# A second gate and up block by seven products instead of eight, with priorities for what it needs first

## The chip, the core and the metric

The kernel runs on one core of a Trainium2 chip. The metric is device time in microseconds (us), here the median of three runs. Beside the times there is one profiled execution; all rows of the profile come from it, in microseconds from the start of its span.

## What is computed

The kernel is one step of a hybrid transformer layer for 128 context tokens and 512 latent tokens, 640 in all, of width 1024. What matters here is its last third, the feed-forward part, for both kinds of tokens:

```python
x = x + g1 * mix
h2 = _rms(x, norm_ffn) * (1 + sc2) + sh2
gate, up = jnp.split(h2 @ w_gate_up, 2, axis=-1)
x = x + g2 * ((jax.nn.silu(gate) * up) @ w_down)
```

The gate and the up projection have 2816 columns each. `mix` is the result of attention and of a short convolution, after an output projection. All of it is in float32.

## The kernel before

**Matmuls in three parts.** A float32 operand is kept as a sum of two tiles: a high part, which ScalarE (ACT) copies into a rounded format (L148, or L1020 for tokens), and a low part, the rest, which VectorE (DVE) subtracts (L149, L1021). TensorE (PE) then multiplies high by high, high by low and low by high (`mm3`, L151 to L154). Making the two parts is called a split.

**Output projection** (L1039 to L1083). Tokens stand in five tiles of 128, the context first (`TORD`). The loop over `j` takes the two halves of the 1024 columns, the inner loop the five token tiles. In the second half, each token tile is added to `x`, normed (`x2n`), and in the next turn transposed by PE (`h2_turn`, L955, L961). The results leave PSUM with the second modulation (L968 on ACT; for the last tile half of them on DVE, L966) and make up `h2`, which has the tokens along its columns.

**Token operands.** `h2` is cut into four quarters: the first digit is the half of the 1024 features, the second the half of the 640 tokens, low (LO) or high (HI), 320 each. B11, B12, B21 and B22 are these quarters, split (`b_plain`). T1 = B12 - B11, T2 = B22 - T1, T3 = B22 - B12 and T4 = B21 - T2 are made of them by DVE (L1034) and split as well (`b_sums`). The high half is made in two pieces: its first 192 columns as soon as their tokens are there, and its last 128 columns (`two[1]`), which belong to the last token tile, later.

**Gate and up blocks.** The feed-forward columns are taken in 22 blocks of 128. For block `f`, A11 and A12 are the gate weights of the two feature halves, A21 and A22 the up weights. Each quarter of the result can be had from two products of a weight operand and a token operand, eight for a block (`plain`, L1103: four for LO, four for HI). Or the block takes seven products, in the manner of Strassen and Winograd: A11·B11, S1·T1, S2·T2, A12·B21, S3·T3, A22·T4 and S4·B22, with the weight sums S1 = A21 + A22, S2 = S1 - A11, S3 = A11 - A21 and S4 = A12 - S2 (`op_load`, L204). A product is twelve matmuls of 128x128 by 320. The first `NPLAIN` blocks (56: two of them) are plain, the others are done in `ff_a` to `ff_e` and `ff_end`: the products accumulate in shared PSUM banks, which ACT copies out in between (L1130), and DVE adds the parts (L1143, L1159, L1162, L1169) and multiplies silu(gate) by up (L1113, L1163, L1171). The texts call the blocks the first (`f` 0), the second (`f` 1), the third (`f` 2) and so on.

**What sets the order.** PE runs its instructions in the order of the program. On the other engines the order is planned when the kernel is built: among the instructions that are ready, the one that comes first in the program is taken, and inside `early(n)` (L144) an instruction counts as if it stood `n` places earlier. Weights come through a planned list (`plan`, L284 to L308): `W(key)`, at each product, also issues the steps that stand up to `AOP` = 9 places further on, so operands are made ahead. They are not issued before their phase (`phase[0]`; 2 up to the start of the blocks, 3 from L1225 on). The raw weights of a block are loaded by SyncE (L222) in two pieces, gate and up, into three buffers (`WFB`); a split operand takes one of four buffers of tag `wh` or of tag `wl`, in turn, and these are shared with the output weights.

The order of the first blocks is written out in L1216 to L1228: the first 192 high columns of the token operands and of their sums; four LO products of the first block; transposes of the last token tile; its columns of B12 and B22; four LO products of the second block; the last columns of T1 to T4; four HI products of each block. From the third block on each runs as `ff_a`, `ff_c`, `ff_end` of the block before, `ff_d`, `ff_b`, `ff_e` (L1229 to L1240).

Of the kernel before, what the change touches and what calls it, by code (L numbers as in the profile page):

```python
# [11 lines left out]
AF = mybir.ActivationFunctionType  # L12
# [6 lines left out]
NL = 4  # L19
# [29 lines left out]
GCUT = [0, 6, 12, 17, 22]  # L49
GB = 3  # L50
SOP = [20, 0]
CPP = 50
GSP = 30
FEND = 2
AOP = 9
NPLAIN = 2
QEV = '00001'
PPO = ''
RSP = 0
# [5 lines left out]
BHD = ("B21", "B22")  # L65
TL = 1
G2N = 0
DSI = 0
PT = 2
PRB = 4  # L70
PHB = 2
# [1 line left out]
BP = 300  # L73
# [15 lines left out]
def build(ctx, tc, x_prompt, x_sample, c, cache_k, cache_v, c_ctx, norm_mix, norm_ffn, w_ada, b_ada,  # L89
# [54 lines left out]
    def early(n):  # L144
        return tc.high_priority(n)
# [46 lines left out]
    def op_load(e):  # L192

        f, name = e[0][1:]
        g, u = (order[place[x, f]][5] for x in "gu")
        a11, a12, a21, a22 = g[:, 0:4], g[:, 4:8], u[:, 0:4], u[:, 4:8]
        if name[0] == "S":
            if name == "S1":
                sums[f] = T("sx", (P, 2, 4, P), F32, 2)
            s13, s24 = sums[f][:, 0], sums[f][:, 1]  # L200
            src, x, y, op = {"S1": (s13, a21, a22, ALU.add), "S2": (s24, s13, a11, ALU.subtract),
                             "S3": (s13, a11, a21, ALU.subtract), "S4": (s24, a12, s24, ALU.subtract)}[name]
            with early(SOP[f >= NPLAIN]):
                (pool if f < SPO else dve).tensor_tensor(src, x, y, op)  # L204
        else:
            src = {"A11": a11, "A12": a12, "A21": a21, "A22": a22}[name]
        w = T(("wh", "wl")[ops[0] % 2], (P, 2, 4, P), F32R, WHB)
        ops[0] += 1
        with early(SOP[f >= NPLAIN]):
            split(w[:, 0], w[:, 1], src)  # L210
        e[5] = w

# [70 lines left out]

    GROUPS = [list(range(a, b)) for a, b in zip(GCUT, GCUT[1:])]  # L284
    PLAIN, PRODS = ("A11", "A12", "A21", "A22"), ("A11", "S1", "S2", "A12", "S3", "A22", "S4")

    def plan_raw(f, x, ph=3):
        col = f * P + (DFF if x == "u" else 0)
# [2 lines left out]
    def plan_ops(f, names, ph=3):  # L291
        for x in names:
            plan(("op", f, x), None, ph, "op")

    G2KP = {0: (0,), 1: (1,), 2: (2, 3)}
    for gi, grp in enumerate(GROUPS):
        for f in grp:
            ph = 2 if f < NPLAIN else 3
            plan_raw(f, "g", ph)
            plan_raw(f, "u", ph)  # L300
            plan_ops(f, PLAIN if f < NPLAIN else PRODS, ph)
        for j in range(2):
            for i0 in range(0, len(grp), 2):
                n = len(grp[i0:i0 + 2])
                plan(("d", grp[i0], j), wd[:, grp[i0]:grp[i0] + n, j * 512:(j + 1) * 512], 2)
                if gi == 0 and j == 0:
                    for kp in G2KP[i0 // 2]:
                        plan(("ada", 5, 1, kp), wa[:, 2 * kp:2 * kp + 2, 5 * D + 512:6 * D], 2, "f")  # L308
# [469 lines left out]
    rA = [None] * NT  # L778
# [119 lines left out]
    def att_rms(t):  # L898
        sps = PB((P, 1))
        for p in range(4):  # L900
            pe.matmul(sps, osq[t][:, p], ones[:, 0:1], start=(p == 0), stop=(p == 3))
        rA[t] = rstd_of(sps, 1, 1.0 / 512, tag="rA")
# [40 lines left out]
    phase[0] = 2  # L943


    if DSI:
        act.activation(warm, warm, AF.Silu)
    h2 = [T("gT", (P, 4, TOK), F32, GB) for _ in range(2)]
    LO, HI = slice(0, HALF), slice(HALF, TOK)
    x2 = [None] * NT  # L950
# [4 lines left out]
    def h2_turn(t):  # L955
        cc = 1 if t == CTX else 0
        for g in range(2):
            tp = PB((P, 4, P))
            for i in range(4):
                k = 4 * g + i  # L960
                pe.transpose(tp[:, i], x2n[t][:, k * P:(k + 1) * P], ident)  # L961
            for i in range(4):
                k = 4 * g + i
                dst, a, b = h2[g][:, i, TS[t]], modA[1][:, k, cc:cc + 1], modB[1][:, k, cc:cc + 1]
                if i >= 4 - H2E[t]:
                    dve.tensor_scalar(dst, tp[:, i], a, b, ALU.mult, ALU.add)  # L966
                else:
                    act.activation(dst, tp[:, i], AF.Identity, bias=b, scale=a)  # L968
# [54 lines left out]
    def b_plain(names, part):  # L1023
        for x in names.split():
            b_put(x, quarter(x, part), part)

    def b_sums(part):
        n = part.stop - part.start
        b11, b12, b21, b22 = (quarter(x, part) for x in ("B11", "B12", "B21", "B22"))
        last = None  # L1030
        for x in ("T1", "T2", "T3", "T4"):
            w = T("tr", (P, 4, 192), F32, 3)[:, :, :n]
            y, z = {"T1": (b12, b11), "T2": (b22, last), "T3": (b22, b12), "T4": (b21, last)}[x]
            dve.tensor_tensor(w, y, z, ALU.subtract)  # L1034
            b_put(x, w, part)
            if x != "T3":
                last = w

    for j in range(2):  # L1039
        cols = slice(j * 512, (j + 1) * 512)  # L1040
        for n, t in enumerate(TORD):
            cc = 1 if t == CTX else 0
            c0 = t * P + (2 if t == CTX else 0)
            ms = [mix_ctx if t == CTX else mix_half(of[t]), mix_half(yf[:, :, c0:c0 + P])]
            ab = PS2()
            for half in range(2):
                for p in range(4):
                    wh, wl = W(("o", j, 2 * half + p // 2))
                    mm3(ab[:, half], ms[half][0][:, p], ms[half][1][:, p], wh[:, p % 2], wl[:, p % 2],
                        p == 0, p == 3)  # L1050
                if j == 0 and CRP == f"{n}{'me'[half]}":
                    next(ada_gen, None)
                    conv_rms()
            if j == 1 and n:
                h2_turn(TORD[n - 1])
                with early(BP):
                    if n == 2:
                        b_plain("B11 B21", slice(0, 256))
                    if n == 3:
                        b_plain("B11 B21", slice(256, HALF))  # L1060
            if j == 0 and n == 1:
                att_rms(NL - 1)
            if j == 0 and G2N <= n < 4 + G2N:
                g2_step(0, n - G2N)
            if j == 1 and n == 0:
                g2_out(0)
            if j == 0:
                x2[t] = T("x2", (P, D), F32, NT)
                sp.dma_start(x2[t], x_dram[t])
            with early(XP[j]):  # L1070
                m = T("mix", (P, 512), F32, 2)
                act.activation(m, ab[:, 1], AF.Copy, scale=rB[t])
                dve.scalar_tensor_tensor(m, ab[:, 0], rA[t], m, ALU.mult, ALU.add)
                e = pool if j == 0 and n < PX else dve
                e.tensor_tensor(m, m, g1[cc][:, cols], ALU.mult)
                e.tensor_tensor(x2[t][:, cols], m, x2[t][:, cols], ALU.add)
            if j == 1:
                with early(XP[j]):
                    x2n[t] = T("x2n", (P, D), F32, 1)
                    ss = T("ss", (P, 1), F32, 6)  # L1080
                    act.activation(x2n[t], x2[t], AF.Square, accum_out=ss)
                    r = rstd_of(ss, 1, 1.0 / D)
                    dve.tensor_scalar_mul(x2n[t], x2[t], r)  # L1083
# [49 lines left out]
    def ff_a(f):  # L1133
        b1 = FB()
        prod(b1, f, "A11", "B11")
        cg = T("cg", (P, TOK), F32, 2)
        st[f] = [b1, copy_of("p1", b1), cg, None, None, None, None]
# [76 lines left out]
    for gi, grp in enumerate(GROUPS):  # L1214
        for f in grp:
            if f == 0:  # L1216
                two = slice(0, 192), slice(192, HALF)
                b_plain("B12 B22", two[0])
                b_sums(two[0])
                for x in range(NPLAIN):  # L1220
                    plain(x, ("B11", "B21"), LO)
                    if x == 0:
                        h2_turn(TORD[-1])
                        b_plain("B12 B22", two[1])
                        phase[0] = 3  # L1225
                b_sums(two[1])
                for x in range(NPLAIN):
                    plain(x, ("B12", "B22"), HI)  # L1228
            elif f >= NPLAIN:  # L1229
                ff_a(f)  # L1230
                if f - 1 in st and FEND == 1:
                    ff_end(f - 1)
                ff_c(f)
                if f - 1 in st:
                    ff_end(f - 1)
                ff_d(f)
                ff_b(f)
                ff_e(f)
                if f == grp[-1] or FEND == 0:
                    ff_end(f)  # L1240
        down(gi, grp)
        for f in grp:
            del gT[f]
# [52 lines left out]
```

## Time and profile before

| | us |
|---|---|
| median of 3 runs | 763.05 |
| lowest, highest | 762.94, 763.66 |
| the profiled execution | 762.58 |
| its span, first to last instruction | 760.8 |

The mean granted clock of TensorE in the profiled execution is 0.996. In the profile a row names the line, the engine, the operation, the tile written and the tiles read, with partitions and elements. In rows of the timeline the first number is the start, the second the duration (of all merged instructions, where a count above 1 stands at the end); in square brackets is the engine's idle time just before and what ended it. A merged row ends with its last instruction. In rows by stretch the first three columns are the stretch and its length, then the busy time of each engine with its number of instructions, then the granted clock of TensorE (1.00 is full), the busy share of the DMA engines and GB/s. An instruction's duration is longer than the distance to the next one where the engine overlaps the two.

### The profile page before, as it was taken

The page shows a single profiled execution, that of the slowest core. Times are in us where ns is not written, and L with a number is a line of the kernel's source. Part 1 is how long each engine was busy: PE and PEld are TensorE (multiplying, and loading weights), DVE is VectorE, ACT ScalarE, POOL GpSimd, SP SyncE. Part 2 cuts the span into 40 slices and gives each one's busy share as a digit, 9 for nine tenths or more (in the row PEclk, how much of TensorE's full clock was granted, in tenths as well). Part 3 has the DMA queues.
Part 4 walks back from the last instruction along what each step waited for, and adds up shares of the span by engine and source line. Part 5 has one row for each costly group of instructions (what it writes and reads, how often), then busy time and mean ns, then how long its engine had stood idle before and what let it go on. Part 6 is the DMA issues. An engine that isn't in the chain of part 4 may idle for free.

```text
span 760.8 us, 11888 instructions
## 1 busy us (share of the span) xinstructions
PE 738.9 (97%) x4580; PEld 662.7 (87%) x4580; DVE 560.1 (74%) x1009; ACT 373.8 (49%) x712; POOL 48.2 (6%) x77
## 2 busy tenths in 40 slices
PE   4999999999999999989999999999999999999997
PEld 3778988989999887789998789998889998899986
DVE  5566987676666798899879678884578866788653
ACT  5455776656665445865552135553125541255410
POOL 3105201011010130000000000000000000000000
PEclk9899999999999999999999999999999999999999
DMA  9994134433424443121325223223113132222312
GB/s 290 298 255 133 44 110 133 133 91 120 144 90 147 153 171 111 35 77 56 110 89 180 82 62 103 83 86 114 52 56 110 58 111 73 67 87 81 112 55 84
DMA packets 102350, 84.52 MB, mean 111 GB/s; under 512 B 4527, under 2 KB 82675, under 8 KB 102293
## 3 DMA queue, kind: packets, MB, share of 16 engines
q1 hardware_dynamic: 100980, 83.39, 36.0%
q8 instruction: 36, 0.59, 0.3%
q10 hardware_dynamic: 1056, 0.26, 0.2%
q0 software_dynamic: 256, 0.11, 0.1%
q14 instruction: 22, 0.17, 0.1%
HBM read 79.68 MB, written 2.75 MB: 108 GB/s over the span
## 4 chain that ended last, share of the span: by engine, by line
PE 81%; DVE 9%; ACT 2%; issue 2%; DMA 2%; SPq 1%; POOL 1%; POOLq 0%; ACTq 0%; DVEq 0%
PE pf L152 17%; PE pf L153 17%; PE pf L154 17%; PE pc L675 3%; PE pc L676 3%; PE pc L677 3%; PE pc L377 2%; PE po L832 2%; PE ps L789 2%; PE pt L815 2%; PE ps L152 2%; PE ps L153 2%; PE ps L154 2%; DMA af<-in_w_ada_dram 1%; POOL rs L162 1%
## 5 line engine op out<-in xcount | busy, mean ns | idle before, releaser
L148 ACT ACTIVATE wh<-wf 128x1024 fp32r<-128x1024 f32 (+1 forms) x76 | 64.1, 843 | 92.0 <-PE pf L154 63.8
L152 PE MATMUL pf<-wh,gT 128*128 128x512 f32 (+1 forms) x225 | 88.0, 391 | 0.0
L153 PE MATMUL pf<-wl,gT 128*128 128x512 f32 (+1 forms) x225 | 87.6, 389 | 0.0
L154 PE MATMUL pf<-wh,gT 128*128 128x512 f32 (+1 forms) x225 | 87.6, 389 | 0.0
L149 DVE TENSOR_TENSOR wl<-wf,wh 128x1024 fp32r<-128x1024 f32 (+1 forms) x42 | 49.2, 1172 | 27.3 <-ACT wh L148 24.4
L675 PE MATMUL pc<-hH,wh 128*128 128x320 f32 x192 | 61.1, 318 | 0.0
L677 PE MATMUL pc<-hH,wl 128*128 128x320 f32 x192 | 59.4, 309 | 0.0
L676 PE MATMUL pc<-hL,wh 128*128 128x320 f32 x192 | 59.3, 309 | 0.0
L153 PEld LDWEIGHTS pf<-wl,gT 128*128 128x128 f32 x225 | 42.2, 187 | 9.9 <-DVE wl L149 0.2
L154 PEld LDWEIGHTS pf<-wh,gT 128*128 128x128 f32 x225 | 42.2, 187 | 9.9
L152 PEld LDWEIGHTS pf<-wh,gT 128*128 128x128 f32 x225 | 42.2, 187 | 9.9 <-ACT wh L148 0.2
L152 PE MATMUL pf<-T,wh 128*128 128x320 f32 x160 | 49.4, 308 | 0.1
L153 PE MATMUL pf<-T,wh 128*128 128x320 f32 x160 | 49.2, 308 | 0.0
L154 PE MATMUL pf<-T,wh 128*128 128x320 f32 x160 | 49.2, 308 | 0.0
L152 PE MATMUL pf<-T,wl 128*128 128x320 f32 x160 | 49.2, 308 | 0.0
L153 PE MATMUL pf<-T,wl 128*128 128x320 f32 x160 | 49.2, 308 | 0.0
L154 PE MATMUL pf<-T,wl 128*128 128x320 f32 x160 | 49.2, 308 | 0.0
L152 PE MATMUL pf<-B,wl 128*128 128x320 f32 x152 | 46.9, 308 | 0.0
L153 PE MATMUL pf<-B,wl 128*128 128x320 f32 x152 | 46.8, 308 | 0.0
L154 PE MATMUL pf<-B,wl 128*128 128x320 f32 x152 | 46.8, 308 | 0.0
L1209 DVE TENSOR_TENSOR dm<-pf,g 128x512 f32<-128x512 f32 (+1 forms) x41 | 27.7, 676 | 23.3 <-PE pf L154 23.3
L148 ACT ACTIVATE wl<-wf 128x512 fp32r<-128x512 f32 x34 | 21.2, 628 | 44.6 <-PE pf L153 36.8
(281 smaller groups left out, 2055.6 us busy)
## 6 DMA issues: line engine op xcount, KB each, us to landing
wf<-in_w_gate_up_dram SPq DMA_DIRECT2D x44, 512.0 KB, 3.8
aw<-in_w_ada_dram SPq DMA_DIRECT2D x24, 512.0 KB, 4.8
wf<-in_w_down_dram SPq DMA_DIRECT2D x20, 512.0 KB, 3.3
wf<-in_w_in_dram SPq DMA_DIRECT2D x18, 512.0 KB, 6.0
af<-in_w_ada_dram SPq DMA_DIRECT2D x32, 256.0 KB, 6.0
x<-in_x_sample_dram SPq DMA_DIRECT2D x8, 512.0 KB, 4.5
wf<-in_w_out_dram SPq DMA_DIRECT2D x8, 512.0 KB, 4.7
wf<-in_w_ada_dram SPq DMA_DIRECT2D x8, 512.0 KB, 3.7
```

What stands on the lines that cost most here:

```text
L148: act.activation(hi, src, AF.Copy)
L149: dve.tensor_tensor(lo, src, f32(hi), ALU.subtract)
L152: pe.matmul(out, lh, rh, start=start, stop=False, skip_group_check=more)
L153: pe.matmul(out, lh, rl, start=False, stop=False, skip_group_check=more)
L154: pe.matmul(out, ll, rh, start=False, stop=stop, skip_group_check=more)
L377: pe.matmul(out[CG * g:CG * (g + 1)], cp[:, k], w, start=(k < 4), stop=(k >= KD - 4), skip_group_check=True)
L675: pe.matmul(acc, wh[:, k], hH[k][:, c0:c0 + n], start=(k == 0), stop=False)
L676: pe.matmul(acc, wh[:, k], hL[k][:, c0:c0 + n], start=False, stop=False)
L677: pe.matmul(acc, wl[:, k], hH[k][:, c0:c0 + n], start=False, stop=(k == KD - 1))
L789: pe.matmul(s2[:, g, :320], q, kk[:, v, P + g * 320:P + (g + 1) * 320], start=(i == 0), stop=(i == 1))
L815: pe.transpose(tp[:, i, h], u[3][h][:, kt * P:(kt + 1) * P], ident)
L1209: dve.tensor_tensor(dm, ps[:, :n], g2[cc][:, oc], ALU.mult)
```

## The change

Only the first block stays plain (`NPLAIN` 1). The second block is done by seven products. Its products A11·B11 and A12·B21 come after the transposes of the last token tile, in place of the second block's LO products; then the first block's HI products; then its other five products. Its operands are made in the order of `FIRST`, and it keeps phase 2 in the plan. Its A11 and A12 are split with `early(300)` (`APP`). The evictions of transposed tokens (L964 to L968) and the last columns of B12 and B22 get `early(300)` (`BP`). `TPP` is 0, so `b_sums` of the first 192 columns keeps its place. Silu is called once on a dummy (`warm`), reading `rA` of the last token tile, in the first half of the output projection.

```diff
+APP = 300
+TPP = 0
-NPLAIN = 2
+NPLAIN = 1
-DSI = 0
...
-        with early(SOP[f >= NPLAIN]):
+        with early(APP if f == NPLAIN and name in ("A11", "A12") else SOP[f >= NPLAIN]):
             split(w[:, 0], w[:, 1], src)
...
+    FIRST = ("A11", "A12", "S1", "S2", "S3", "A22", "S4")
...
-            ph = 2 if f < NPLAIN else 3
+            ph = 2 if f <= NPLAIN else 3
             plan_raw(f, "g", ph)
             plan_raw(f, "u", ph)
-            plan_ops(f, PLAIN if f < NPLAIN else PRODS, ph)
+            plan_ops(f, PLAIN if f < NPLAIN else FIRST if f == NPLAIN else PRODS, ph)
...
-    if DSI:
-        act.activation(warm, warm, AF.Silu)
...
             for i in range(4):
+              with early(BP):
                 k = 4 * g + i
...
                 att_rms(NL - 1)
+                act.activation(warm, rA[NL - 1], AF.Silu)
...
                 b_plain("B12 B22", two[0])
-                b_sums(two[0])
+                with early(TPP):
+                    b_sums(two[0])
                 for x in range(NPLAIN):
                     plain(x, ("B11", "B21"), LO)
                     if x == 0:
                         h2_turn(TORD[-1])
-                        b_plain("B12 B22", two[1])
+                        with early(BP):
+                            b_plain("B12 B22", two[1])
                         phase[0] = 3
+                ff_a(NPLAIN)
+                ff_b(NPLAIN)
                 b_sums(two[1])
                 for x in range(NPLAIN):
                     plain(x, ("B12", "B22"), HI)
             elif f >= NPLAIN:
-                ff_a(f)
+                if f > NPLAIN:
+                    ff_a(f)
...
                 ff_d(f)
-                ff_b(f)
+                if f > NPLAIN:
+                    ff_b(f)
                 ff_e(f)
```

## The prediction

> **What bounds the kernel now.** I read the page first, then the busy time by stages, then TensorE's (PE's) gaps, then VectorE's (DVE's) list.
>
> ```profile
> PE 738.9 (97%) x4580; PEld 662.7 (87%) x4580; DVE 560.1 (74%) x1009; ACT 373.8 (49%) x712; POOL 48.2 (6%) x77
> PE 81%; DVE 9%; ACT 2%; issue 2%; DMA 2%; SPq 1%; POOL 1%; POOLq 0%; ACTq 0%; DVEq 0%
> ```
>
> PE is busy 97% of the span and is 81% of the chain that ended last. But the chain leaves PE for DVE and ScalarE (ACT) just where the gate and up blocks begin, so that stage is looked at alone.
>
> ```profile
> core 0: us, PE busy (x) PEld busy (x) DVE busy (x) ACT busy (x) POOL busy (x), PEclk, DMA share, GB/s
> 320.00:332.00 12.00, 11.05 (x78) 10.73 (x78) 10.99 (x19) 10.34 (x22) 0.55 (x1) 1.00 0.48 141
> 332.00:345.00 13.00, 10.80 (x72) 10.31 (x71) 12.85 (x23) 6.75 (x13) 0.00 (x0) 1.00 0.13 32
> 345.00:357.00 12.00, 12.00 (x84) 12.00 (x83) 11.17 (x19) 6.49 (x13) 0.00 (x0) 1.00 0.30 87
> 370.00:385.00 15.00, 15.00 (x105) 15.00 (x104) 12.75 (x22) 8.14 (x17) 0.00 (x0) 1.00 0.24 72
> ```
>
> The two regimes are what the reader is to see. From 345 on PE is full. From 332 to 345 it is DVE that is full (12.85 of 13.00 us), and PE loses 2.2 us. Here DVE makes the lower parts of all token operands (B12, B22, T1 to T4) and the operands of the next blocks. Before, the second block's eight plain products give DVE cover for this: the first use of a T comes with the third block.
>
> ```profile
> 321.69 0.66 PE L961 MATMUL pt<-ident,x2n 128*128 128x128 f32 x4 [0.63 <-ACT gT L968]
> 322.10 0.39 PE L152 MATMUL pf<-B,wh 128*128 128x320 f32 x1
> 330.02 0.39 PE L152 MATMUL pf<-B,wh 128*128 128x320 f32 x1
> 339.19 0.41 PE L152 MATMUL pf<-gT,wh 128*128 128x320 f32 x1 [1.89 <-ACT gT L1020]
> 346.91 0.31 PE L152 MATMUL pf<-gT,wh 128*128 128x320 f32 x1
> 353.95 0.31 PE L152 MATMUL pf<-B,wh 128*128 128x320 f32 x1
> 355.71 0.31 PE L152 MATMUL pf<-T,wl 128*128 128x320 f32 x1
> ```
>
> These are starts: first block's low columns 322.10, second block's low columns 330.02, the first block's high columns 339.19, the second's 346.91, third block 353.95. A product (twelve matmuls) is 355.71 - 353.95 = 1.76 us, four are 7.04. I follow the start of the third block: PE is full after it, so what it moves, the end moves.
>
> **The change part by part.** *One product fewer:* 1.76 us saved on PE.
>
> *Evictions of transposed tokens first.* The gap of 0.63 us at 321.69 waits for evictions that stood behind operand splits; it goes. The large one is the last token block: PE has transposed it by about 330.1, but the evictions come late.
>
> ```profile
> 329.07 1.28 ACT L1112 ACT_TABLE_LOAD   x1
> 334.68 0.44 ACT L968 ACTIVATE gT<-pt,modB,modA 128x128 f32<-128x128 f32 x1
> 335.76 1.15 ACT L968 ACTIVATE gT<-pt,modB,modA 128x128 f32<-128x128 f32 x3
> 337.69 1.36 DVE L966 TENSOR_SCALAR gT<-pt,modA,modB 128x128 f32<-128x128 f32 x4
> 339.17 0.69 DVE L1021 TENSOR_TENSOR gT<-gT,gT 128x512 fp32r<-128x512 f32 x1
> ```
>
> With priority they run right after 330.1 (1.6 us of ACT and 1.36 of DVE beside each other), then the last columns of B12 and B22 (0.69 us and less each): ready at about 333. The high columns now start at 332.9 (below), so nothing of the old wait is left. It was 339.19 less the 337.06 at which the four products from 330.02 are issued, 2.13 us, and the slow first product (346.91 - 339.19 - 7.04) another 0.68: 2.8 us saved. What was done late on DVE is only done earlier; its amount stays.
>
> *Silu's table.* The 1.28 us load moves to the first half of the output projection.
>
> ```profile
> 272.04 0.63 ACT L148 ACTIVATE mH<-of 128x512 fp32r<-128x512 f32 x1 [2.49 <-PE ps L153]
> 274.80 0.64 ACT L148 ACTIVATE mH<-y 128x512 fp32r<-128x512 f32 x1 [2.12 <-PE ps L153]
> ```
>
> ACT idles over 2 us there before each split and hides it: nothing. The bound is 1.3 us, if a split behind it came late. At 329 it held no one that PE waited for: nothing saved either.
>
> *PE without a stall.* Low columns start at 322.10 - 0.63 = 321.47; four products to 328.51; the transposes with their gap 0.87 (330.02 - 322.10 - 7.04 rounded); A11 and A12 of the second block from 329.4 to 332.9; the first block's four high products to 339.9; five products of the second block 8.8, to 348.7. Saved are 1.76 + 0.63 + 2.8 = 5.2 us.
>
> *A new bubble.* The second block's A12·B21 is moved ahead, so S3·T3 follows S2·T2 directly, into the same bank that ACT must first copy out.
>
> ```profile
> 359.81 0.44 ACT L1130 ACTIVATE u<-pf 128x320 f32<-128x320 f32 x1 [1.07 <-PE pf L154]
> ```
>
> The copy is 0.44 us; with the last matmul's tail (0.31 less its 0.15 of issue) and two hand-overs, 0.66 us. In the other blocks A12·B21 covers it.
>
> *The work of seven products on DVE.* This is the term that decides. S1·T1 of the second block now wants all of T1 and its own S1 at 339.9. DVE's list of before up to there:
>
> ```profile
> 340.11 0.69 DVE L204 TENSOR_TENSOR sx<-wf 128x512 f32<-128x512 f32 x1
> 341.31 0.69 DVE L204 TENSOR_TENSOR sx<-sx,wf 128x512 f32<-128x512 f32 x1
> 341.92 0.49 DVE L1113 TENSOR_TENSOR cu<-pf,cg 128x320 f32<-128x320 f32 x1
> 342.32 0.69 DVE L1034 TENSOR_TENSOR tr<-gT 128x512 f32<-128x512 f32 x1
> 343.65 0.68 DVE L1034 TENSOR_TENSOR tr<-gT,gT 128x512 f32<-128x512 f32 x1
> 344.25 0.68 DVE L149 TENSOR_TENSOR wh<-wf,wh 128x512 fp32r<-128x512 f32 x1
> 344.85 1.28 DVE L1021 TENSOR_TENSOR T<-tr,T 128x512 fp32r<-128x512 f32 x2
> 325.71 0.15 DVE L160 TENSOR_SCALAR ms<-ss 128x1 f32<-128x1 f32 x1 [0.35 <-ACT x2n L1081]
> 326.52 0.75 DVE L1083 TENSOR_SCALAR x2n<-x,rs 128x1024 f32<-128x1024 f32 x1 [0.66 <-POOL rs L162]
> ```
>
> Start to start, an operation of 512 elements takes 0.60 us and one of 320 takes 0.40. T1's last lower part is done at 344.85 + 0.69 = 345.5. Of what precedes it, the new order doesn't need: A21's split 0.6, the third block's two sums 1.2, L1113 of the second block 0.4, T3's difference 0.6: 2.8. It has on top: four sums 2.4, the splits of S1 to S4 2.4, L1143 0.4: 5.2. The third block's A11 stands in both, since its place in the program is ahead of these last columns, as is that of S1 to S4. So 345.5 + 2.4 = 347.9, less up to 1.0 for the idle time at 325 and 326 which some of it may fill, less 0.6 if T2's difference follows: 346.2 to 347.9. I take 346.6. In the worst case the third block's S1 comes first as well (1.2 more). So PE stands from 339.9 to 346.6: 6.7 us, and all later products stand in its queue behind S1·T1; ACT's copies of their banks wait in turn. The other lower parts (six more steps, 3.6 us) are then in time.
>
> *L1159.* S4·B22 adds to a bank that DVE must have read. DVE is then behind with the third block's operands: between nothing and three of these steps, 1.8; I take 0.6.
>
> *DMAs.* The third block's raw up half can be loaded only when A22 of the second is split and its slot free, later than the 328.51 of before.
>
> ```profile
> 328.51 0.37 SPq L222 DMA_DIRECT2D wf<-in_w_gate_up_dram  x1
> wf<-in_w_gate_up_dram SPq DMA_DIRECT2D x44, 512.0 KB, 3.8
> ```
>
> If A22 is split by about 340, it lands by 344; S1 of the third block is wanted after 353. Nothing, as long as SyncE's queue holds nothing ahead of it: the down blocks come later.
>
> *The clock.* The trace shows what a thin stretch costs.
>
> ```profile
> 15.00:16.00 1.00, 0.00 (x0) 0.00 (x0) 1.00 (x3) 1.00 (x3) 0.00 (x0) 1.00 1.17 310
> 17.00:18.00 1.00, 0.26 (x4) 0.23 (x8) 0.80 (x5) 0.22 (x2) 0.09 (x1) 0.83 1.20 290
> 18.00:19.00 1.00, 0.82 (x8) 0.00 (x0) 0.51 (x1) 0.97 (x2) 1.00 (x2) 0.50 1.20 290
> 23.00:24.00 1.00, 1.00 (x6) 0.80 (x5) 0.00 (x0) 0.00 (x0) 0.00 (x0) 0.50 1.20 267
> 20.56 0.80 PE L152 MATMUL ps<-wh,hH 128*128 128x512 f32 x1
> 22.44 0.63 PE L153 MATMUL ps<-wl,hH 128*128 128x512 f32 x1
> 24.98 0.39 PE L153 MATMUL ps<-wl,hH 128*128 128x512 f32 x1
> ```
>
> PE is idle from 15 to 16 and busy for a quarter of 17 to 18; the granted clock falls to 0.50 and is still there at 23 to 24, over 3 us after dense matmuls began at 20.56 (they last 0.63 us at 22.44 and 0.39 at 24.98). Half of 3.4 to 3.8 us is lost, 1.7 to 1.9; if the stall is cut in pieces, nothing. Taken: 1.5. The Trainium skill, "TensorE: Matmul & The Clock Gate", section "What's actually happening", says that an idle window of about 3.4 us halves the array's clock and that a busy one restores it. That speaks against a stall of this length; its estimate, half a window, is 1.7 us where I took 1.5, and the trace agrees that a thin stretch of about 3 us suffices.
>
> *Sum.* 6.7 + 0.66 + 0.6 + 1.5 - 5.2 = +4.3 us, of which I keep 4.2. The profiled execution took 762.58 us (span 760.8), 0.47 below the median 763.05; the forecast is 763.05 + 4.2 = 767.2.
>
> **Rivals.** *Smaller stall:* the clock doesn't fall and L1159 is in time: 6.7 + 0.66 - 5.2 = +2.2, 765.2. *Larger:* the evictions aren't moved forward on the engines' lists, or S1 of the third block goes first: 1.2 to 2.8 more, 768.4 to 770.0.
>
> *Faster: DVE in the order of need.* If S1, T1, S2, T2 and so on come in the order in which PE wants them, only the total counts: 346.6 - 0.6 (A11 of the third) + 3.6 + 0.4 (L1159) = 350.0 for the last operand; PE then starts S4·B22 at 350.1 and the third block at 351.9, 2.05 earlier: 761.0. It decides in the stretch 334 to 346: if the last columns' T1 is done before 342.5, the sum turns negative. For it: DVE picks by priority among what is ready, and slots may hold S3 and S4 back. Against it: in the list of before the third block's sums at 340.11 do go ahead of the differences at 342.32.
>
> *No stall at all:* 5.2 - 0.66 = 4.5 saved, 758.5. That needs DVE to do 6 us of work in no time. PE has the highest share on the page and a product is taken from it. "Perfetto Trace Analysis" of the Trainium skill, section "Identifying the Most-Contended Engine", would have the engine of highest occupancy optimised first, and by that the product is won; the rows of 332 to 345 speak against it.
>
> **How the numbers follow.** The measurement of this kernel can tell about 0.2%, 1.5 us, from no change. Forecast 0.44, smaller stall 0.22, larger 0.08: slower 0.74. Between, where gains and stall meet (761.5 to 764.6): 0.10. DVE in order of need 0.12, no stall 0.04: faster 0.16. The likeliest case's own range is 765.5 to 769.0. The range for 8 in 10 takes the unknown costs at their upper ends (1.2 for S1, 1.2 more on L1159, 0.4 of clock: 770) and reaches down to the best order: 760.8 to 770.2.
>
> **What would show it.** PE idle some 6 us before the second block's S1·T1, released by DVE's T L1021 or by a wh/wl split; PEclk at 0.50 just after; a gap of 0.6 before S3·T3, released by ACT's u L1130; no wait at the first block's high columns; DVE full from 320 to 355; the table load at about 272. No PE gap before S1·T1 would make the prediction wrong, and so would a DVE list that has T1's last columns ahead of S3 and S4. Twelve matmuls fewer must be there in any case.

## The result, and the profile after

The changed kernel takes 772.39 us (median of 4 runs, 768.17 to 774.25) against 763.0 before: ratio 1.0098, 95% interval 1.0075 to 1.0121. The direction was forecast, the size was not: +9.4 us by the medians against +4.2, above the range. By the ratio, which takes all runs, it is 0.98%, 7.5 us (one of the four runs is far below the others); the experiments are compared by their ratios. The profiled execution took 772.51 us, its span is 770.6 (before 760.8), its mean granted clock 0.987 (before 0.996). The other three runs: 768.17 us at 0.997, 772.27 at 0.987, 774.25 at 0.985.

From the page, the busy time of TensorE (PE) to GpSimd, and the chain that ended last:

```profile
PE 744.0 (97%) x4568; PEld 668.4 (87%) x4568; DVE 565.3 (73%) x1020; ACT 376.8 (49%) x719; POOL 48.5 (6%) x77
PE 84%; DVE 6%; ACT 3%; DMA 2%; SPq 2%; issue 1%; POOL 1%; ACTq 0%; DVEq 0%; POOLq 0%
```

There are twelve matmuls fewer, yet PE is busy 5.1 us longer (744.0 for 738.9): its matmuls last longer. From here on lines of the changed kernel are one or two higher than before. PE in the timeline, from the first block's low columns to the third block:

```profile
323.37 0.39 PE L153 MATMUL pf<-B,wh 128*128 128x320 f32 x1
...
330.49 1.03 PE L961 MATMUL pt<-ident,x2n 128*128 128x128 f32 x8
331.28 0.39 PE L153 MATMUL pf<-B,wh 128*128 128x320 f32 x1
...
334.74 0.31 PE L155 MATMUL pf<-B,wl 128*128 128x320 f32 x1
337.78 0.64 PE L153 MATMUL pf<-gT,wh 128*128 128x320 f32 x1 [2.73 <-ACT gT L1021]
338.80 0.64 PE L154 MATMUL pf<-gT,wh 128*128 128x320 f32 x1 [0.39 <-DVE gT L1022]
...
348.17 0.30 PE L155 MATMUL pf<-B,wl 128*128 128x320 f32 x1
351.11 0.55 PE L153 MATMUL pf<-T,wh 128*128 128x320 f32 x1 [2.64 <-ACT T L1021]
352.26 0.64 PE L154 MATMUL pf<-T,wh 128*128 128x320 f32 x1 [0.59 <-DVE T L1022]
...
358.19 0.31 PE L155 MATMUL pf<-T,wl 128*128 128x320 f32 x1
359.03 0.41 PE L153 MATMUL pf<-T,wh 128*128 128x320 f32 x1 [0.53 <-ACT u L1132]
...
364.42 0.31 PE L153 MATMUL pf<-B,wl 128*128 128x320 f32 x1
```

The reader is to see two stalls where one was forecast: before the first block's high columns (337.78), and before the second block's S1·T1 (351.11). The clock, by stretches of the same kernel:

```profile
337.78:345.00 7.22, 6.83 (x26) 6.48 (x27) 6.58 (x10) 2.17 (x4) 0.00 (x0) 0.54 0.01 2
345.00:351.00 6.00, 3.47 (x24) 3.21 (x22) 4.50 (x9) 3.14 (x6) 0.00 (x0) 1.00 0.60 174
351.00:358.50 7.50, 6.80 (x24) 6.19 (x24) 6.33 (x11) 3.53 (x7) 0.00 (x0) 0.54 0.00 1
```

After each stall the clock is at half for 6.8 us (337.58 to 344.40 and 351.23 to 358.06). The account of the 9.8 us between the spans, all from these rows, with 0.147 us as the distance of two matmuls and 1.76 us as a product (a "late lower part" is the second, short wait, for the part of the operand that DVE makes):

| | us |
|---|---|
| before the low columns: a clock fall at 75 to 78 us and smaller shifts | +1.6 |
| gap at the last but one transposes gone (0.33 of it net) | -0.33 |
| one product fewer | -1.76 |
| the stall of before at the high columns, 2.13, its slow product, 0.68, rest | -2.83 |
| gap 334.89 to 337.78, and a late lower part, 0.39 | +3.28 |
| gap 348.32 to 351.11, and a late lower part, 0.59 | +3.38 |
| half clock: 48 matmuls in 10.54 instead of 7.04, 24 in 7.23 instead of 3.52, less 0.98 of late lower parts | +6.2 |
| bubble before S3·T3 (358.34 to 359.03) | +0.69 |
| slow first matmuls | +0.2 |
| from the third block on | -0.6 |

The first row isn't the change's. Up to 78 us both kernels run the same instructions in the same order on PE, ACT and GpSimd, and on DVE but for a swap near 9 us, with the same thin stretch from 66 to 74 us. Here the stretch of 75 to 78 us in the changed kernel, then in the kernel before:

```profile
75.00:78.00 3.00, 3.00 (x14) 3.00 (x14) 2.49 (x7) 2.97 (x11) 1.95 (x1) 0.50 0.00 0
```

```profile
75.00:78.00 3.00, 3.00 (x25) 3.00 (x25) 2.41 (x8) 2.97 (x10) 1.95 (x1) 1.00 0.00 0
```

Of the profiles below, e2, e3 and e8 show a fall at this place too, the others don't. It may be part of why the runs of one kernel lie 6 us apart; only the profiled ones show it.

Why the high columns come late: ScalarE (ACT), then VectorE (DVE), in the timeline of the changed kernel.

```profile
330.23 0.42 ACT L1114 ACTIVATE cg<-pf 128x320 f32<-128x320 f32 x1
333.10 0.63 ACT L149 ACTIVATE wl<-sx 128x512 fp32r<-128x512 f32 x1 [2.44 <-DVE sx L205]
333.63 1.49 ACT L969 ACTIVATE gT<-pt,modB,modA 128x128 f32<-128x128 f32 x4
...
344.99 0.63 ACT L149 ACTIVATE wl<-wf 128x512 fp32r<-128x512 f32 x1 [2.69 <-PE pf L155]
```

```profile
332.38 0.69 DVE L205 TENSOR_TENSOR sx<-sx,wf 128x512 f32<-128x512 f32 x1
...
335.92 1.36 DVE L967 TENSOR_SCALAR gT<-pt,modA,modB 128x128 f32<-128x128 f32 x4
...
346.50 0.69 DVE L150 TENSOR_TENSOR wh<-sx,wh 128x512 fp32r<-128x512 f32 x1 [2.14 <-ACT wh L149]
...
349.71 0.68 DVE L1035 TENSOR_TENSOR tr<-gT 128x512 f32<-128x512 f32 x1
350.31 0.69 DVE L205 TENSOR_TENSOR sx<-wf 128x512 f32<-128x512 f32 x1
```

The transposes are done at about 331.5, but ACT idles 2.44 us with the split of the second block's S2 at the head of its queue. That split waits for S2's sum, which DVE starts at 332.38; the evictions stand behind it, priority or not. The DVE half of them starts still later, at 335.92, behind other vector work. Later, DVE itself idles 2.14 us before 346.50, behind a split of ACT (344.99) that waits for a slot which PE's half-speed products hold. So T1's last columns are begun only at 349.71. One slow queue makes the next one slow. Through both waits of PE, DVE is busy without a pause (3.41 of 3.41 us in 334.17 to 337.58, and again in 347.82 to 351.23).

### The profile page after: what moved, and what is told of

The parts are those of the page before. It is cut to its first block, busy times and chain, and to the rows that moved or that the text cites. A ratio compares the mean times of both kernels' runs of the same rounds, so it can differ in the third digit from the quotient of the medians.

```text
span 770.6 us, 11879 instructions
## 1 busy us (share of the span) xinstructions
PE 744.0 (97%) x4568; PEld 668.4 (87%) x4568; DVE 565.3 (73%) x1020; ACT 376.8 (49%) x719; POOL 48.5 (6%) x77
## 4 chain that ended last, share of the span: by engine, by line
PE 84%; DVE 6%; ACT 3%; DMA 2%; SPq 2%; issue 1%; POOL 1%; ACTq 0%; DVEq 0%; POOLq 0%
PE pf L154 19%; PE pf L155 18%; PE pf L153 18%; PE pc L677 3%; PE pc L678 3%; PE pc L679 3%; PE ps L791 2%; PE po L834 2%; PE pt L817 2%; PE pc L379 2%; PE ps L153 2%; PE ps L154 2%; DMA af<-in_w_ada_dram 2%; PE ps L155 2%; SPq L323 1%
## 5 line engine op out<-in xcount | busy, mean ns | idle before, releaser
L153 PE MATMUL pf<-T,wh 128*128 128x320 f32 x168 | 52.5, 312 | 3.2 <-ACT T L1021 2.6
L154 PE MATMUL pf<-T,wh 128*128 128x320 f32 x168 | 52.5, 312 | 0.6 <-DVE T L1022 0.6
L155 PE MATMUL pf<-T,wh 128*128 128x320 f32 x168 | 52.3, 311 | 0.0
L153 PE MATMUL pf<-T,wl 128*128 128x320 f32 x168 | 52.3, 311 | 0.0
L154 PE MATMUL pf<-T,wl 128*128 128x320 f32 x168 | 52.2, 311 | 0.0
L155 PE MATMUL pf<-T,wl 128*128 128x320 f32 x168 | 52.1, 310 | 0.0
L149 ACT ACTIVATE wl<-sx 128x512 fp32r<-128x512 f32 x41 | 25.8, 628 | 51.1 <-PE pf L154 35.7
L153 PE MATMUL pf<-B,wl 128*128 128x320 f32 x140 | 43.6, 311 | 0.0
L155 PE MATMUL pf<-B,wl 128*128 128x320 f32 x140 | 43.5, 311 | 0.0
L154 PE MATMUL pf<-B,wl 128*128 128x320 f32 x140 | 43.5, 311 | 0.0
```

The source lines that it names most:

```text
L149: act.activation(hi, src, AF.Copy)
L153: pe.matmul(out, lh, rh, start=start, stop=False, skip_group_check=more)
L154: pe.matmul(out, lh, rl, start=False, stop=False, skip_group_check=more)
L155: pe.matmul(out, ll, rh, start=False, stop=stop, skip_group_check=more)
```

## The experiments

The theories: **D**, the amount of vector work of seven products, more than there is time for; **Q**, the order of the in-order queues, which puts operands not yet needed ahead of the evictions; **K**, the clock, which falls after the stalls. Other rivals are spelled out where they are expected. All ratios are against runs of the kernel before on the same chip.

| | median us (runs) | before | ratio, 95% interval |
|---|---|---|---|
| e1 priorities alone | 761.31 (10) | 764.1 | 0.9966, 0.9953 to 0.9979 |
| e2 seven products alone | 771.24 (4) | 764.1 | 1.0097, 1.0074 to 1.0120 |
| e3 last sums early | 772.03 (4) | 764.1 | 1.0090, 1.0056 to 1.0124 |
| e4 waits filled | 769.61 (4) | 764.1 | 1.0068, 1.0050 to 1.0087 |
| e5 sums on GpSimd | 769.68 (4) | 764.1 | 1.0079, 1.0059 to 1.0099 |
| e6 sum operands late | 769.59 (4) | 763.91 | 1.0078, 1.0051 to 1.0106 |
| e7 no sums | 766.65 (10) | 763.91 | 1.0039, 1.0024 to 1.0055 |
| e8 e1, copies earlier | 762.3 (10) | 763.91 | 0.9976, 0.9965 to 0.9988 |
| e9 e6, evictions on ACT | 767.0 (6) | 764.24 | 1.0038, 1.0020 to 1.0056 |
| e10 e1, splits in place | 761.2 (5) | 764.24 | 0.9965, 0.9952 to 0.9978 |
| e11 e9, B21 and B22 on ACT | 767.42 (4) | 764.24 | 1.0046, 1.0030 to 1.0063 |
| e12 e9, no sums | 765.27 (10) | 763.51 | 1.0022, 1.0001 to 1.0043 |

**e1, the priorities and Silu's call alone**, with two plain blocks:

```diff
+              with early(BP):
...
+                        with early(BP):
                             b_plain("B12 B22", two[1])
...
+                act.activation(warm, rA[NL - 1], AF.Silu)
```

> Both first blocks plain as before; only the priorities of the evictions and of the last columns, and Silu's early load. Theory D (the seven products bring vector work that the first products then wait for): without them the wait of 2.1 us at the first block's high columns and that of 0.6 us at the last transposes shrink, and the time falls by 2 to 3.4 us to 759.6 to 761. Rival C (the priorities themselves push needed splits back): no gain, 763 to 768.

Measured: 2.8 us faster than before, as D has it, though 761.31 is just over its 759.6 to 761. PE at the high columns, then ACT at the evictions:

```profile
336.42 0.31 PE L154 MATMUL pf<-B,wl 128*128 128x320 f32 x1
336.57 0.31 PE L152 MATMUL pf<-gT,wh 128*128 128x320 f32 x1
```

```profile
329.39 0.46 ACT L1114 ACTIVATE cg<-pf 128x320 f32<-128x320 f32 x1
329.71 1.54 ACT L969 ACTIVATE gT<-pt,modB,modA 128x128 f32<-128x128 f32 x4
```

The evictions run at once and the high columns follow without a gap. From the first block to the third it is 29.19 us instead of 31.85, and the low columns begin 0.64 earlier: 3.3 us, as the prediction's 0.63 and 2.8. Some of it is given back, here on PE, then on ACT:

```profile
355.78 0.42 PE L152 MATMUL pf<-T,wh 128*128 128x320 f32 x1 [1.45 <-ACT p L1132]
```

```profile
354.67 0.74 ACT L148 ACTIVATE gT<-cu 128x640 fp32r<-128x640 f32 x1 [1.32 <-DVE cu L1115]
355.31 0.42 ACT L1132 ACTIVATE p<-pf 128x320 f32<-128x320 f32 x1
```

The copy of the third block's A11·B11 stands behind a split that waits for DVE, which is without an idle moment there.

**e2, the seven products alone**: the changed kernel without the priorities, with `APP = 0` and without Silu's call.

> Seven products for the second block, no priorities, Silu not moved. Theory D: as slow as the change or slower, 772 to 776, with a longer wait at the first block's high columns. Rival C: most of the loss is gone, 763 to 766.

```profile
344.05 0.64 PE L153 MATMUL pf<-gT,wh 128*128 128x320 f32 x1 [8.36 <-ACT gT L1020]
```

Measured +7.1 us, a little under the theory's 772. PE waits 8.36 us in one piece, and S1·T1 then comes without a wait. The ratio is that of the whole change (1.0097 and 1.0098). So the seven products are the loss, and the priorities, worth 2.8 us with two plain blocks, are worth nothing that shows here: they only cut the wait in two. The rival falls.

**e3, the order of need**: the last columns of T1 to T4 get priority as well.

```diff
-                b_sums(two[1])
+                with early(BP):
+                    b_sums(two[1])
```

> The change, and the last columns of T1 to T4 get the priority of 300 as well. Theory D with the order of the vector list as its core: the wait at S1 times T1 shrinks from 2.6 us plus 0.6 to under 1, and the time falls to 767 to 770. Rival (only the amount of vector work counts): the wait moves to S2, S3 or S4, and the time stays at 771 to 773.

Measured: ratio 1.0090, which can't be told from the changed kernel's 1.0098. The wait at S1·T1 is gone, that at the high columns is unchanged (2.73 and 0.39), and a new one stands in the third block, on PE, and behind it DVE's wait for a load:

```profile
373.32 0.43 PE L153 MATMUL pf<-B,wl 128*128 128x320 f32 x1 [2.43 <-DVE cu L1161]
```

```profile
367.50 0.69 DVE L205 TENSOR_TENSOR sx<-wf 128x512 f32<-128x512 f32 x1 [0.98 <-DMA wf<-in_w_gate_up_dram]
```

The second block's S3 and S4 are now made later, so its raw weights hold their buffers longer: the next loads are issued at 353.3 and 354.5 instead of 344.4 and 347.8, and the third block's operands are late. The wait has moved, with a fall of the clock (0.83 from 370 to 380). The order of need doesn't remove it, against the prediction's faster rival. The time is that of the rival here (771 to 773), not the theory's 767 to 770.

**e4, the waits filled** with 18 unused matmuls before the high columns and 18 before S1·T1, 36 x 0.147 = 5.3 us of PE:

```diff
+                filler(18)
                 b_sums(two[1])
...
+                else:
+                    filler(18)
```

> The change, with 18 extra matmuls (2.6 us at full clock) into an unused bank ahead of the first block's high products, and 18 ahead of S1 times T1, where the array stood idle; their result is not used. Theory K (about 4 us of the loss is the halved clock after these waits): the granted clock stays above 0.995 in the profile, and the time falls to 767 to 769 in spite of 5.3 us of extra work. Rival (the clock costs little, since the vector engine sets the pace anyway): 771 to 775.

```profile
332.00:345.00 13.00, 11.25 (x78) 11.02 (x76) 13.00 (x21) 7.20 (x14) 0.00 (x0) 1.00 0.01 1
345.00:351.00 6.00, 5.31 (x37) 5.04 (x35) 5.32 (x11) 2.79 (x6) 0.00 (x0) 1.00 0.64 174
351.00:357.00 6.00, 4.17 (x23) 3.43 (x23) 6.00 (x11) 3.53 (x7) 0.00 (x0) 1.00 0.00 1
```

Measured 769.61: just over K's 767 to 769 and under the rival's 771 to 775. The clock holds (1.00 in all three stretches), and with 5.3 us more to do the ratio is 0.30% lower, 2.3 us; the two intervals overlap from 1.0075 to 1.0087. DVE is then full in 332 to 345 (13.00 of 13.00) and in 351 to 357 (6.00 of 6.00), which points to DVE's queue as the bound once the clock holds.

**e5, the second block's sums on GpSimd** (`SPO = 2`, which moves the sums of blocks below 2).

> The change, with the second block's four weight sums on GpSimd (1.62 us for one operation of this size there by the profile, against 0.60 on the vector engine). Theory D (amount of vector work): 2.4 us less on the vector engine, the waits ahead of the first high columns and of S1 times T1 shrink by about as much, 767 to 770. Rival Q (the order in the queues counts, not the amount): the scalar engine still stands before a split of a sum that now comes later still, and the time is 771 to 775.

Measured 769.68, inside D's 767 to 770 and under the rival's 771 to 775; but by ratio, 1.0079, it is 0.19% under the changed kernel, within the intervals, so it decides nothing between the two. Pieces of wait stay at the high columns (2.03 and 1.12) and S1·T1 (0.79 and 0.73), and one arises on the way:

```profile
330.36 1.09 PE L961 MATMUL pt<-ident,x2n 128*128 128x128 f32 x8 [1.92 <-DVE x2n L1085]
```

The last transposes now wait 1.92 us for `x2n`. What DVE was rid of did not come back as time that can be told from none.

**e6, the operands of the second block's S1 to S4 not before phase 3**, so behind the evictions:

```diff
+            if f == NPLAIN:
+                plan_ops(f, FIRST[:2], ph)
+                plan_ops(f, FIRST[2:], 3)
```

> The change, but S1, S2, S3, A22 and S4 of the second block are issued only after the last tokens' evictions. Theory Q (the evictions came late since the scalar engine stood before the split of S2, whose sum the vector engine had not made): the evictions start within 0.5 us of the transposes, the wait of 2.7 us at the first high columns goes, and with it the first fall of the clock: 765 to 769, with a wait of 3 us or more left ahead of S1 times T1. Theory D alone (amount): the wait only moves to S1 times T1, 770 to 773.

ACT's evictions start at 329.73, no split ahead of them. DVE and then PE:

```profile
332.97 0.95 DVE L1039 TENSOR_TENSOR tr<-gT,gT 128x768 f32<-128x768 f32 x1
...
334.71 1.35 DVE L971 TENSOR_SCALAR gT<-pt,modA,modB 128x128 f32<-128x128 f32 x4
```

```profile
336.24 0.42 PE L153 MATMUL pf<-gT,wh 128*128 128x320 f32 x1 [2.59 <-ACT gT L1025]
...
349.50 0.41 PE L154 MATMUL pf<-T,wh 128*128 128x320 f32 x1 [2.00 <-DVE T L1026]
```

Measured 769.59, between Q's 765 to 769 and D's 770 to 773: ratio 1.0078, 0.20% under the changed kernel, again within the intervals; from the first block to the third it is 39.33 us for 41.05. The wait at the high columns, which Q has gone, is there (2.59 us): DVE's half of the evictions stands behind sums of the tokens' first columns. Q as told of ACT alone is not the whole.

**e7, the second block's four weight sums left out** (its S1 to S4 are split from raw weights): 2.4 us less on DVE, and nothing for the splits to wait for.

> The change without the second block's four weight sums: its products S1 to S4 take raw weight blocks, so this block's result is another. Theory D: 2.4 us of vector work and the chains through the sums are gone; the waits shrink to under 2 us in all, the clock mostly holds, 763 to 767. Rival (the tokens' sums alone are late enough): 769 or more.

Measured: ratio 1.0039, 0.59% under the changed kernel, 4.5 us for 2.4 us of vector work, and outside its interval. 766.65 is inside D's 763 to 767, but not by D's way: the waits are 2.03, 0.31, 1.68 and 1.65, 5.67 us where D has under 2 and the changed kernel 6.35. What is much shorter is the half clock, 3.4 us in this stage of the profile instead of 13.7, which is worth 5.1 us. So D is borne out only in part: the sums cost, but by the profiles most of what they cost comes through the clock, and the splits are also freed of a wait, so some of Q is in it.

**e9, e6 with all eight last evictions on ACT** (`H2E` all 0), and **e12, e9 without the four sums**.

> The kernel e6 (the sum operands of the second block in phase 3) with the last token tile's evictions all on ScalarE, none on VectorE. Theory (in e6 the wait of 2.6 us at the first block's high columns is that of the VectorE half of the evictions, which stands behind vector work; ScalarE is free from 329.7): eight evictions of 0.4 us end at about 333.2, the wait at the high columns is under 1 us, VectorE has 1.4 us less, the waits at the second block's S1 T1 stay at 1 to 3 us; no fall of the clock before the high columns; 766 to 768.5. Rival (the lower parts of B12 and B22, on VectorE, are what comes late, whoever evicts): a wait of 2 us and more stays at L154 of the high columns, released by VectorE, and 769 to 770.

> e9 (sum operands of the second block late, last evictions on ScalarE) without the second block's four weight sums: its S1 to S4 are split from raw weights, so that block's result is another. 2.4 us less on VectorE, and ScalarE isn't ahead of anything. Theory (once the evictions stand behind nothing, what is left of the loss is the amount of vector work up to the second block's last operand): 2 to 3.5 us faster than e9's 767.0, 763.5 to 765; the wait at L154 of the high columns 2.7 us or less (one sum of 0.6 less ahead of it). Rival (the seven products' order of operands, not the amount): no more than 1 us faster than e9.

e9 in the timeline, ACT, DVE and PE:

```profile
330.06 2.21 ACT L973 ACTIVATE gT<-pt,modB,modA 128x128 f32<-128x128 f32 x6 [0.41 <-PE pt L965]
```

```profile
334.17 0.95 DVE L1039 TENSOR_TENSOR tr<-gT,tr 128x768 f32<-128x768 f32 x1
...
336.64 0.68 DVE L1026 TENSOR_TENSOR gT<-gT,gT 128x512 fp32r<-128x512 f32 x1
```

```profile
337.38 0.41 PE L154 MATMUL pf<-gT,wh 128*128 128x320 f32 x1 [3.26 <-DVE gT L1026]
```

The time is the theory's (767.0, ratio 1.0038), the mechanism the rival's: the evictions end at 333.5, yet PE waits 3.26 us for the lower part of B12, which DVE starts at 336.64, behind two sums of the first columns (1.7 us) and three further operations. The wait has gone from the eviction to the subtraction behind it. By ratio e9 is 0.60%, 4.6 us, under the changed kernel. e12 is 0.16%, 1.2 us, under e9, within the intervals; from the low columns to the third block its profile has 33.84 us instead of 35.56. These 1.7 us are no more than what e9's profile loses to 3.41 us at half clock, where e12's has none (the rows stand in the last section). So 765.27 is short of the theory's 763.5 to 765, and what the sums are worth apart from the clock isn't shown. The 3.26 us wait is the same in e12: where e9 has a sum and a difference of T just ahead of the subtraction, e12 has two splits, as long.

**e11, e9 with the high parts of B21 and B22 on ACT** (`BHD = ()`).

> e9 with the high parts of B21 and B22 made by ScalarE instead of VectorE: five operations fewer on VectorE in the stage, about 1.5 to 2.5 us. Theory (the amount of vector work before the second block's last operand sets the loss): 2 us and more faster than e9, near 764 to 766, and not faster than the kernel before with the priorities alone (761). Rival (what is left is the order of the queues, not the amount): as e9 within 1 us.

Measured 767.42, as e9 within 1 us: the rival's number, and its reason, the queues. ACT and PE:

```profile
333.52 1.71 ACT L1025 ACTIVATE T<-tr 128x768 fp32r<-128x768 f32 x2 [3.61 <-DVE tr L1039]
335.14 2.19 ACT L973 ACTIVATE gT<-pt,modB,modA 128x128 f32<-128x128 f32 x6
```

```profile
337.90 0.63 PE L153 MATMUL pf<-gT,wh 128*128 128x320 f32 x1 [4.09 <-ACT gT L1025]
```

The plan has shifted a little, ACT again has an operand at its head that waits (for T sums, 3.61 us), the evictions come at 335.14, and PE waits 4.09 us. What DVE gained, the queue took.

**e8 and e10, e1 with its last wait attacked**: the copies 300 places earlier (`CPP = 300`); the first two blocks' result splits on their places instead of 30 earlier.

> Two plain blocks with the priorities alone, and the scalar engine's copies out of the shared banks get a priority of 300 for 50. The profile of the priorities alone has one wait of 1.45 us left, at S2 times T2 of the third block, for the first such copy. If that copy was only planned too late, the wait goes: 1.0 to 1.5 us below the kernel with the priorities alone, 759.8 to 760.5. If the copy waits for something else, no difference: 761 to 762.

> The priorities alone (e1, two plain blocks) with the splits of the first two blocks' results on their places instead of 30 places earlier. Theory (in e1 the wait of 1.45 us at the third block's S2 T2 is that for ScalarE's copy of A11 B11, which stands behind the split of the second block's result, and that split waits for VectorE): the wait goes, PE has no gap between 322 and 360, 0.8 to 1.5 us faster than e1: 759.8 to 760.6. Rival (the copy only finds the next thing to stand behind): 761 to 762, and a wait of over 1 us at the third block.

762.3 and 761.2: no gain over e1, and e8 is over both of the ranges that were expected of it. In both the wait before S2·T2 stays (1.45 us): the split, which waits for DVE, still stands ahead of the copy on ACT. For e10 that is the rival's case. What beats the kernel before and the changed one is e1, 0.34% faster than before (interval 0.21% to 0.47%); e10 can't be told from it.

## Why the prediction missed, step by step

- **One product fewer, 1.76; Silu's table.** Right: 4568 matmuls, and the load stands in idle ACT time:

```profile
271.20 1.28 ACT L1064 ACT_TABLE_LOAD   x1
274.49 0.20 ACT L1064 ACTIVATE warm<-rA 128x1 f32<-128x1 f32 x1 [2.01 <-POOL rA L163]
```

- **"With priority they run right after 330.1 … nothing of the old wait is left."** This step failed first. It holds with two plain blocks (e1). With seven products, operands of S1 to S4, in phase 2, stand ahead of the evictions. The order is fixed when the kernel is built; in the run a queue waits for its head, whatever the priority of those behind it. The rival "larger" named this and was given 0.08 and 1.2 to 2.8 us; its 768.4 to 770.0 still falls short of 772.39. Nothing was gained on the old wait of 2.8 us: one of 3.28 us stands in its place.
- **The stall of 6.7 us at S1·T1.** DVE's work as its cause is supported (DVE is full through the waits, and e7 takes away 4.5 us, by the profiles most of it through the clock); its amount and its order weren't told apart. Waits add up to 3.28 + 3.38 = 6.66 us, but in two places, and the agreement is partly luck: in e2 it is one wait of 8.36, and in the changed kernel half-speed products cover some vector work and hold back other.
- **The clock, "if the stall is cut in pieces, nothing. Taken: 1.5".** The step with the largest miss, 6.2 us in the profiled execution. Two pieces of 2.7 and 2.6 us each brought 6.8 us at half clock. It need not be 6.2 in the time, as the half-speed products also cover vector work: e4, where the clock holds, is 2.3 us faster, and the one run of the changed kernel at a mean clock of 0.997 is 4.1 and 4.3 us below the two at 0.987 (with the fall at 75 us perhaps among it). By that one run the change costs about 5 us without falls, where the prediction's sum without the clock was 2.7. The Trainium skill, "TensorE: Matmul & The Clock Gate", section "What's actually happening", has an idle window of about 3.4 us bring the half clock: 2.73 and 2.64 us sufficed here, while 1.45 (e1), 1.75 (e4) and, in e12, 3.26 us didn't.
- **The bubble, 0.66**: 0.69 measured. **L1159, 0.6**: no wait there in the changed kernel.
- **DMAs, "Nothing"**: so in the changed kernel. In e3 the same buffers, freed later, made DVE wait 0.98 us ahead of PE's wait of 2.43: the cover was thin.
- **DVE in the order of need, 761.0**: e3, the nearest to it, gained nothing; by its rows, because what is put back holds buffers that the next block needs.

Of the 0.98%, mending the order (e9) takes back 0.60, falls of the clock among it; taking the sums away as well (e12) 0.16 more, which is within the intervals. What the last 0.22 (interval 0.01 to 0.43) consists of was not taken apart: in e12's profile PE still waits 3.3 us at the high columns and 1.8 at S1·T1. How much of e9's gain is order and how much clock stays open too: in the profiles the stage has 13.7 us at half clock in the changed kernel, 3.4 in e9 and none in e12, worth 6.8, 1.7 and 0 us, and neither e9's 4.6 us nor e12's 1.2 is more than the difference. Not tried: an order of DVE written out by hand for this stage.

## What to carry to other kernels

Where an engine beside TensorE is full in a stage, taking a product away there is likely to gain only if the operands of the cheaper scheme cost that engine no more than the product saved, here 1.76 us against 5.2 us of vector work (565.3 less 560.1). A priority orders what is ready, and an in-order queue still waits for its head: so find, for each instruction that is to be early, the last one ahead of it that waits for another engine. And price each stall of about 2 us and more with what the clock may do after it: here nothing, 1.7 or 3.4 us (5.1 in e2), by where the stall lies and whether another follows.

## What the runs showed of the hardware

The granted clock fell after waits of 2.64 and 2.73 us and stayed at half for 6.8 us. In e9 it fell after one of 3.26 us for a shorter time, in e6 after one of 2.00 us in the second block, and in e7 once after two waits of 1.68 and 1.65 us, 2.1 us apart (half from 348.76 to 352.18). In e12 a wait of 3.26 us, like that of e9, brought no fall.

The clock records of the traces say more than the means: in every profile each fall that ends within the span lasts 3.41 us or two or three times that, and the falls of one execution begin whole multiples of 3.41 us apart. So the row of these equal stretches can be drawn through an execution. Here are the stretches around the wait in e9, and then in e12:

```profile
334.99:338.40 3.41, 1.02 (x7) 1.02 (x8) 3.41 (x7) 2.37 (x5) 0.00 (x0) 1.00 0.00 0
338.40:341.81 3.41, 3.41 (x15) 3.41 (x15) 3.41 (x7) 1.16 (x2) 0.00 (x0) 0.50 0.02 5
```

```profile
332.49:335.91 3.42, 1.73 (x12) 1.47 (x11) 3.42 (x6) 3.11 (x7) 0.00 (x0) 1.00 0.00 0
335.91:339.32 3.41, 1.83 (x12) 1.79 (x13) 3.41 (x7) 1.55 (x4) 0.00 (x0) 1.00 0.02 5
```

The same wait lies mostly in one stretch in e9, where PE is busy for 1.02 of 3.41 us, and is shared by two in e12. From 320 to 380 us in the profiles of the changed kernel and of all experiments, half clock followed every stretch at full clock in which PE was busy for 46% or less (26% and 23% in the changed kernel), and none of 57% or more; between the two, 49% (e4), 51% and 54% (e12) brought no fall and 56% (e5) did. The half clock went on for another stretch where PE still waited in the first one (busy 83% of it in both falls of the changed kernel, for the late lower parts), and ended after one where PE was busy all through (e5, e7, e9). So what a fall costs doesn't follow the length of the wait: it comes in steps, 1.7 us for each stretch at half clock. This doesn't explain the thin stretch from 66 to 74 us: PE was busy for 68% of the stretch before the changed kernel's fall at 74.75, and for 68% of one in e7 that brought none.
